# Attention: the four attended tiles of the 13th head's block are split in front of its softmax instead of behind it

## The chip, the cores and the metric

The kernel runs on one core of a Trainium2 chip. The metric is the device time of one execution in microseconds; lower is better. Five engines share the work, and each takes its own instructions strictly in the order in which they were written: PE (TensorE, matrix multiplies, with its weight loads shown as PEld), DVE (VectorE, elementwise), ACT (ScalarE, elementwise with functions), POOL (GpSimd) and SP (SyncE, which here issues DMAs). They wait for each other through semaphores.

## The reference, cut to what matters

Two layers run over a sequence of 1024 positions of width 1024: a gated short convolution with a dense SwiGLU network behind it, then dilated attention with another SwiGLU network. The change touches the attention layer alone.

```
BRANCHES = ((128, 1), (512, 4), (2048, 16))
def dilated_attention_mixer(h, w_qkv, w_out, rel_bias):
    qkv = (h @ w_qkv).reshape(bsz, seq, 3, N_HEADS, HEAD_DIM)
    for window, dilation in BRANCHES:
        o, l = dilated_branch(q, k, v, rel_bias, window, dilation)
    alpha = jax.nn.softmax(jnp.stack(lses, axis=0), axis=0)
    o = jnp.sum(alpha[..., None] * jnp.stack(outs, axis=0), axis=0)
    return o.reshape(bsz, seq, D_MODEL).astype(h.dtype) @ w_out
```

There are 16 heads of 64 columns. The last line, the product of the attended values with `w_out`, is what the four tiles of the change are for.

## The kernel before, in words

Everything is kept transposed: a tile has 128 rows of the model's width and 1024 positions, so eight tiles make the residual stream, and two heads make one tile of attended values. Products are taken to nearly fp32 accuracy from three faster ones: each operand is split into a high part, which ACT rounds off (line 143, `w_hi<-oin` for an attended tile), and a low part, which DVE makes by subtraction (line 144, `w_lo<-oin,w_hi`). PE then multiplies high by high, low by high and high by low (lines 371, 372 and 373).

The attention runs in 17 slots, `slot(n, ...)` for n = 0 to 16. Slot n computes the scores of head n (PE lines 1569 and 1570, with the bias added by DVE in lines 1580 to 1611 and the running maximum `m` in lines 1594 to 1620), hands `m` to POOL, which reduces it over the partitions (line 1623, `mb<-m`), subtracts that maximum from the score tiles on DVE (line 1631) and takes exponentials on ACT (line 1632). The values of head n-1 (PE line 1642, from score tiles `lf`, `lh`, `ld`, `lp` and the value tile `vx`) are computed in the same slot, and ACT evicts their sums (lines 1665 and 1666, `z` and `o`). Between these small products stand dense ones, drawn one by one from a generator by the inner function `other`: first the value projections (`v`, PE lines 1512 to 1514, ACT line 1517), the query and key projections, and at the end `out_product`, the product of `w_out` with the attended tiles 0 to 3.

An attended tile is finished by DVE (line 1707), written to memory by POOL (line 1708, `odram`), and read back by SP into a tile `oin` (line 1793). At the start of slot 12, which is the 13th head's, `load_attended` issues the four loads, and the generator `halves` splits one tile each time that it is advanced; it is given to `slot` as `hook`. The second half of a slot is a loop over eight steps i. In slots up to 13 the softmax (lines 1631 and 1632) is written in step 3, the maximum over the partitions having been asked for at the end of the first half; the copies `kca` of the next head's keys (ACT line 1553) are written in steps 1 and 2.

The value tiles of a group of heads take a detour: ACT evicts `v` (line 1517), POOL writes it to memory (line 1521, `vdram<-v`), and SP reads it back in another layout into the single tile `vx` (lines 1529 and 1531). The last `v` of the last group is evicted in slot 12, and `vx` with its data is first used by the values of head 12 in slot 13. The order of all instructions is written out by hand through these loops; there is no scheduler behind it. Buffers of one page come from a ring of 41.

Of the kernel before, what the change touches and what calls it, by code (L numbers as in the profile page):

```python
# [46 lines left out]
SOFT = 4  # L47
# [52 lines left out]
def trunk(ctx: ExitStack, tc: tile.TileContext, x, gains_in, cwi, ck, cwo, wqkv, wo, relb,  # L100
# [8 lines left out]
    def page(name, dt=F32):  # L109
        return pages.tile([128, 1024], dt, name=name, tag="page", bufs=PAGES)  # L110
# [265 lines left out]
    def run(*gens):  # L376
        for _ in zip(*gens):
            pass
        for g in gens:
            for _ in g:  # L380
                pass
# [1078 lines left out]
    def load_bias(h):  # L1460
        t = scope["pool"].tile([128, L1 + L2], F32, name="bias", tag="bias", bufs=2)
        base = tables.offset + h * G3
        nc.sync.dma_start(t[:, 0:L1], bass.AP(tensor=tables.tensor, offset=base, ap=[[1, 8], [A1, 16], [1, L1]]))
        nc.sync.dma_start(t[:, L1:L1 + L2], bass.AP(tensor=tables.tensor, offset=base + G0,
                                                    ap=[[1, 32], [A2, 4], [1, L2]]))
        return t
# [8 lines left out]
    def attention(norm, qk):  # L1475
# [58 lines left out]
        def load_kq(n):  # L1534

            p, a = divmod(n, 2)
            k, q = qk.kq[p, 1], qk.kq[p, 0]
            rows = lambda t, r: bass.AP(t.tensor, t.offset + r * S, [[S, 64], [1, S]])
            n0, n1 = (slice(64 * i, 64 * i + 64) for i in (a, 1 - a))
            KS[n], QS[n] = page("ka", F32R), page("qa", F32R)  # L1540
            nc.sync.dma_start(KS[n][n0].bitcast(F32), rows(k, 64 * a))
            nc.sync.dma_start(KS[n][n1].bitcast(F32), rows(k, 128 + 64 * a))
            if n <= LAG + 1 and n % 2 == 0 and n:
                load_values(p - 1)
            for m in (n0, n1):
                nc.sync.dma_start(QS[n][m].bitcast(F32), rows(q, 64 * a))
            nc.sync.dma_start(qlo[a][n0].bitcast(F32), rows(q, 128 + 64 * a))

        def classes(n):

            KC[n] = page("kca", F32R)
            for h in range(2):
                nc.scalar.activation(KC[n][:, half(h)], view(KS[n], h * HALF, [[1, 4], [4, 128]]), AF.Copy)
                yield
# [80 lines left out]
        def values(p, a, st):  # L1635
            lf, lh, ld, lp = (st[n] for n in ("lf", "lh", "ld", "lp"))
            acc = [bank(), bank()]
            kd = [[128, 4], [1, 32]]
            b1 = [[32, 16], [1, 8]]

            def mm(ih, off, dims, u, rhs, first=False, last=False):
                nc.tensor.matmul(view(acc[ih], off, dims), vx[:, u, 64 * a:64 * a + 128], rhs,  # L1642
                                 start=first, stop=last)

            for ih in range(2):
                for r4 in range(4):
                    mm(ih, r4 * 32, kd, 8 + r4, view(lf, ih * HALF + r4 * 32, kd), first=r4 == 0)
                    if r4 % 2:
                        yield
            for r4 in range(4):  # L1650
                mm(1, r4 * 32, kd, 12 + r4, view(lh, r4 * 32, kd))
                if r4 % 2:
                    yield
            for j in range(8):
                off = (j % 4) * 8
                mm(j // 4, off, b1, j, view(ld, blk(j), b1), last=False)
                if j:
                    mm(j // 4, off, b1, j - 1, view(lp, blk(j), b1), last=j % 4 == 3)
                yield
            o, z = st["o"], st["z"]  # L1660
            n0 = slice(64 * a, 64 * a + 64)
            z0 = slice(64 - 64 * a, 128 - 64 * a)
            for ih in range(2):
                s = slice(ih * HALF, (ih + 1) * HALF)
                nc.scalar.activation(z[n0, s], acc[ih][z0], AF.Ln)
                nc.scalar.activation(o[n0, s], acc[ih][n0], AF.Copy)
            yield

        def finish(p):

            o, z = OZ.pop(p)
            if p < NPAIR - 1:
                nc.scalar.activation(z, z, AF.Exp, scale=-1.0)
                put_off.append((p, o, z))
                return
                yield

            acts[p] = page("o_hi", F32R), page("o_lo", F32R)

            def scaled(h):  # L1680
                nc.vector.tensor_tensor(out=o[:, half(h)], in0=o[:, half(h)], in1=z[:, half(h)], op=ALU.mult)

            def parts(h):
                split(o[:, half(h)], [t[:, half(h)] for t in acts[p]])

            def rest():
                parts(1)

            nc.scalar.activation(z[:, half(0)], z[:, half(0)], AF.Exp, scale=-1.0)
            scaled(0)  # L1690
            parts(0)
            yield
            nc.scalar.activation(z[:, half(1)], z[:, half(1)], AF.Exp, scale=-1.0)
            scaled(1)
            nc.scalar.activation(scratch, eps, AF.Sqrt)
            yield
            last_part.append(rest)
            yield
            ensure(ahead_ao + KT - AO_WIDE)
            ensure(ahead_ao + KT - AO_WIDE + 4)  # L1700
            yield
# [11 lines left out]
        def slot(n, dense, ndense, late=0, hook=iter(())):  # L1713

            def other(k):
                for _ in range(k):
                    next(dense, None)

            p, a = divmod(n, 2)
            if n < H:  # L1720
                new = dict(bias=bias.pop(n))
                sc = scores(p, a, new)
            else:
                sc = iter(())
            if n + 1 < H:
                load_kq(n + 1)
                bias[n + 1] = load_bias(n + 1)
            if n:
                q, b = divmod(n - 1, 2)
                if b == 0:  # L1730
                    OZ[q] = page("o"), page("z")
                old = live.pop(n - 1)
                old.update(o=OZ[q][0], z=OZ[q][1])
                pv = values(q, b, old)
            else:
                pv = iter(())
            extra = later = iter(())
            lagged = n <= LAG
            if n + 1 < H:
                later = classes(n + 1)  # L1740
            if lagged and a and p:
                ending.append(finish(p - 1))
            used = 0
            if lagged:
                for i in range(8):
                    next(sc, None)
                    if n or i % 2:
                        other(1)
                        used += 1
                    if a and ending and i == 0:  # L1750
                        run(ending.pop())
                run(sc)
            else:
                if a == 0 and not late:
                    other(1)
                    used += 1
                for i in range(8):
                    next(sc, None)
                    next(pv, None)
                    next(pv, None)  # L1760
                    if i >= late and i % 2 == 0:
                        other(1)
                        used += 1
                run(sc)
                run(pv)
                if a == 0:
                    extra = finish(p - 1)
                if a == 0 and n < H:
                    load_values(p)
            left = max(ndense - used, 0)  # L1770
            for i in range(8):
                next(pv, None)
                next(pv, None)
                if i == (2 if n > LAG + 1 else 5):
                    attended()
                if not lagged and (i < FIN0 or i > SOFT):
                    next(extra, None)
                if i in (1, 2):
                    next(later, None)
                if i == (3 if lagged else SOFT):  # L1780
                    if n < H:
                        live[n] = new
                        run(softmax(new))
                if i >= SOFT:
                    next(hook, None)
                other(left * (i + 1) // 8 - left * i // 8)
            run(pv)
            run(extra)
# [45 lines left out]
        def halves():  # L1834
            for q, t in done.items():
                first[q] = split(t)
                yield

        dense = fill()
        for n in range(H):  # L1840
            if n == LAG - 1:
                done.update(load_attended(range(AO)))
            hook = halves() if n == LAG - 1 else iter(())
# [206 lines left out]
```

## Time and profile before

| | us |
|---|---|
| median of 3 runs | 2130.8 (2130.04 to 2131.32) |
| the profiled execution, its own time | 2129.8 |
| its span, from the first to the last instruction | 2128.0 |
| PE busy | 2102.3 (99%) |
| DVE busy | 1739.8 (82%) |
| ACT busy | 1015.7 (48%) |
| POOL busy | 234.4 (11%) |
| mean granted TensorE clock, as a share of full speed | 0.996 |

All views below are of this one execution, and their times are microseconds from its first instruction. A row of the view in order of time gives the start, the duration, the engine, the line, the operation with the tiles it writes and reads, the shapes and how many instructions were merged; in square brackets stands the idle time of the engine ahead of it and what ended that. An engine that is 99% busy can still be slowed: a busy PE may run at half its clock, and the table by stretches shows the clock that was granted.

### The profile page before, as it was taken

The numbers are of one execution on the slowest core, as the hardware profiler recorded it, in microseconds if no ns is written. First come the engines' busy times: TensorE is split into PE (matmuls) and PEld (weight loads), VectorE is DVE, ScalarE is ACT, GpSimd is POOL, SyncE is SP. The second block draws the span as 40 slices with busy tenths as digits, with TensorE's granted clock in tenths as the row PEclk, the third lists the DMA queues.
The fourth block names the chain that finished last, engine by engine and source line by source line (L and its number), as shares of the span: only waits on it lengthen the run. The fifth ranks groups of instructions, "written<-read, shape, count | busy, mean of one in ns | idle before, by whom it ended". The sixth has DMA issues, their size and how long they took to land.

```text
span 2128.0 us, 30922 instructions
## 1 busy us (share of the span) xinstructions
PE 2102.3 (99%) x11082; PEld 1806.5 (85%) x11082; DVE 1739.8 (82%) x3262; ACT 1015.7 (48%) x1861; POOL 234.4 (11%) x335
## 2 busy tenths in 40 slices
PE   9999999999999999999999999999999999999998
PEld 7888888888888888887899999888788888888887
DVE  8898769988888888878967687787998888888876
ACT  7333426443444554445545545554544444456435
POOL 1000000110101000010322322111011101001000
PEclk9999999999999999999999999999999999999999
DMA  7332642323333566351767767745223233358432
GB/s 219 94 94 70 228 134 75 104 100 109 114 101 108 162 208 211 108 168 40 250 208 186 182 182 211 216 164 152 64 85 109 101 108 114 105 195 241 157 95 79
DMA packets 141464, 300.78 MB, mean 141 GB/s; under 512 B 48188, under 2 KB 54414, under 8 KB 141312
## 3 DMA queue, kind: packets, MB, share of 16 engines
q1 hardware_dynamic: 107488, 201.94, 31.5%
q0 software_dynamic: 26192, 82.17, 11.9%
q10 hardware_dynamic: 7632, 14.70, 1.8%
q8 instruction: 88, 1.44, 0.3%
q14 instruction: 64, 0.52, 0.1%
HBM read 208.48 MB, written 82.93 MB: 137 GB/s over the span
## 4 chain that ended last, share of the span: by engine, by line
PE 85%; DVE 7%; ACT 3%; DMA 2%; issue 2%; POOL 1%; SPq 0%; DVEq 0%; ACTq 0%; POOLq 0%
PE bank L574 19%; PE bank L572 19%; PE bank L573 19%; PE bank L373 4%; PE bank L372 4%; PE bank L371 4%; PE bank L664 3%; PE bank L667 3%; PE bank L666 3%; PE bank L1642 2%; POOL mb L1623 1%; PE bank L1512 1%; PE bank L1513 1%; PE bank L1514 1%; DVE w L144 1%
## 5 line engine op out<-in xcount | busy, mean ns | idle before, releaser
L572 PE MATMUL bank<-b,w 128*128 128x512 f32 x1952 | 764.0, 391 | 2.2 <-ACT w L143 1.8
L574 PE MATMUL bank<-b,w 128*128 128x512 f32 x1952 | 762.0, 390 | 3.6 <-DVE w L144 3.5
L573 PE MATMUL bank<-b,w 128*128 128x512 f32 x1952 | 761.4, 390 | 0.4 <-DVE b L883 0.3
L574 PEld LDWEIGHTS bank<-b,w 128*128 128x128 f32 x1952 | 366.9, 188 | 83.9 <-DVE w L144 7.4
L572 PEld LDWEIGHTS bank<-b,w 128*128 128x128 f32 x1952 | 367.2, 188 | 78.9 <-ACT w L143 2.9
L573 PEld LDWEIGHTS bank<-b,w 128*128 128x128 f32 x1952 | 367.1, 188 | 76.3 <-DVE b L883 1.1
L143 ACT ACTIVATE w<-combo 128x512 fp32r<-128x512 f32 (+2 forms) x488 | 249.1, 540 | 230.2 <-DVE combo L191 213.3
L144 DVE TENSOR_TENSOR w<-combo,w 128x512 fp32r<-128x512 f32 (+2 forms) x488 | 277.7, 583 | 37.6 <-ACT w L143 36.9
L578 ACT ACTIVATE part<-bank 128x512 f32<-128x512 f32 x186 | 110.8, 596 | 390.0 <-PE bank L574 386.6
L144 DVE TENSOR_TENSOR w<-raw,w 128x512 fp32r<-128x512 f32 (+2 forms) x342 | 189.5, 576 | 37.5 <-ACT w L143 37.5
L582 DVE TENSOR_TENSOR part<-part,bank 128x256 f32<-128x256 f32 (+1 forms) x366 | 171.5, 500 | 31.1 <-PE bank L574 16.6
L143 ACT ACTIVATE w<-raw 128x512 fp32r<-128x512 f32 (+2 forms) x342 | 166.9, 530 | 44.4 <-PE bank L574 11.5
L371 PE MATMUL bank<-w_hi,w 128*128 128x512 f32 (+1 forms) x400 | 153.4, 384 | 3.8 <-ACT w_hi L143 3.7
L372 PE MATMUL bank<-w_lo,w 128*128 128x512 f32 (+1 forms) x400 | 149.8, 375 | 1.2 <-DVE w_lo L144 1.2
L373 PE MATMUL bank<-w_hi,w 128*128 128x512 f32 (+1 forms) x400 | 149.8, 375 | 0.7 <-DVE w L144 0.7
L493 DVE TENSOR_TENSOR x<-x,bank 128x512 f32<-128x512 f32 (+1 forms) x104 | 66.4, 644 | 62.6 <-PE bank L373 61.4
L802 DVE TENSOR_TENSOR x<-x,bank 128x512 f32<-128x512 f32 x136 | 93.2, 685 | 29.1 <-PE bank L574 29.1
L191 DVE TENSOR_TENSOR combo<-raw 128x512 f32<-128x512 f32 (+1 forms) x172 | 111.7, 649 | 0.0
L371 PEld LDWEIGHTS bank<-w_hi,w 128*128 128x128 f32 x400 | 75.8, 190 | 17.1 <-ACT w_hi L143 3.9
L372 PEld LDWEIGHTS bank<-w_lo,w 128*128 128x128 f32 x400 | 75.9, 190 | 14.9 <-DVE w_lo L144 2.0
L373 PEld LDWEIGHTS bank<-w_hi,w 128*128 128x128 f32 x400 | 75.6, 189 | 14.7 <-DVE w L144 1.6
L565 DVE TENSOR_TENSOR b<-hin,b 128x512 fp32r<-128x512 f32 x126 | 79.7, 689 | 9.3 <-ACT b L564 9.3
(243 smaller groups left out, 3467.1 us busy)
## 6 DMA issues: line engine op xcount, KB each, us to landing
hin<-part SPq DMA_DIRECT2D x126, 256.0 KB
raw<-in_ffn_w_gate SPq DMA_DIRECT2D x44, 512.0 KB
raw<-in_ffn_w_up SPq DMA_DIRECT2D x44, 512.0 KB
part<-sum POOLq DMA_DIRECT2D x72, 256.0 KB, 2.3
raw<-in_ffn_w_down SPq DMA_DIRECT2D x48, 384.0 KB
raw<-in_attn_w_qkv SPq DMA_DIRECT2D x27, 512.0 KB
raw<-in_conv_w_in SPq DMA_DIRECT2D x24, 512.0 KB
part<-part POOLq DMA_DIRECT2D x36, 256.0 KB, 2.4
```

The costliest lines, as they stand in the source:

```text
L143: nc.scalar.activation(hi, src, AF.Copy)
L144: eng.tensor_tensor(out=lo, in0=src, in1=hi, op=ALU.subtract)
L191: eng.tensor_tensor(out=c, in0=a, in1=b, op=op)
L371: nc.tensor.matmul(b, whi[:, a], ahi[:, s], start=first, stop=False)
L372: nc.tensor.matmul(b, whi[:, a], alo[:, s], start=False, stop=False)
L373: nc.tensor.matmul(b, wlo[:, a], ahi[:, s], start=False, stop=last)
L572: nc.tensor.matmul(b, hi[:, a], bhi, start=start and k == 0, stop=False, skip_group_check=True)
L573: nc.tensor.matmul(b, hi[:, a], blo, start=False, stop=False, skip_group_check=True)
L574: nc.tensor.matmul(b, lo[:, a], bhi, start=False, stop=k == n - 1, skip_group_check=True)
L578: nc.scalar.activation(t, b, AF.Copy)
L582: nc.vector.tensor_tensor(out=t, in0=t, in1=b, op=ALU.add)
L802: nc.vector.tensor_tensor(out=X[n][:, half(h)], in0=X[n][:, half(h)], in1=b, op=ALU.add)
```

## The change

In the second half of slot 12 the four splits are no longer written in steps 4 to 7, behind the softmax that is written in step 3, but in steps 0 to 3, and in step 3 ahead of the softmax. `hook` is an empty iterator in all other slots, so nothing else is moved.

```
@@ -1777,12 +1777,12 @@
                     next(extra, None)
                 if i in (1, 2):
                     next(later, None)
+                if i < 4:
+                    next(hook, None)
                 if i == (3 if lagged else SOFT):
                     if n < H:
                         live[n] = new
                         run(softmax(new))
-                if i >= SOFT:
-                    next(hook, None)
                 other(left * (i + 1) // 8 - left * i // 8)
```

PE, POOL and SP execute the same instructions in the same order as before. On ACT, in slot 12, the copies `w_hi<-oin` are the high parts of the four attended tiles, `kca<-ka` the key copies for the next head, line 1632 the exponentials, and `v<-bank,r` the eviction of the last value tile. Before:

```order
L1517 ACTIVATE v<-bank,r 128x256
L1553 ACTIVATE kca<-ka 128x512 x2
L1632 ACTIVATE lf<-lf 128x1024
L1632 ACTIVATE lh<-lh 128x512
L1632 ACTIVATE ld<-ld 128x1024
L1632 ACTIVATE lp<-lp 128x16x24
L1632 ACTIVATE lp<-lp 128x512
L143 ACTIVATE w_hi<-oin 128x1024
L1517 ACTIVATE v<-bank,r 128x256
L143 ACTIVATE w_hi<-oin 128x1024 x2
L1665 ACTIVATE z<-bank 64x512
```

The same place on ACT, now:

```order
L1517 ACTIVATE v<-bank,r 128x256
L143 ACTIVATE w_hi<-oin 128x1024
L1553 ACTIVATE kca<-ka 128x512
L143 ACTIVATE w_hi<-oin 128x1024
L1553 ACTIVATE kca<-ka 128x512
L143 ACTIVATE w_hi<-oin 128x1024 x2
L1632 ACTIVATE lf<-lf 128x1024
L1632 ACTIVATE lh<-lh 128x512
L1632 ACTIVATE ld<-ld 128x1024
L1632 ACTIVATE lp<-lp 128x16x24
L1632 ACTIVATE lp<-lp 128x512
L1517 ACTIVATE v<-bank,r 128x256
```

All four high parts moved ahead of the exponentials, two of them between the key copies; the eviction of `v` now follows the last exponential directly. The fourth high part stood, before, behind the evictions `z` and `o` of head 11's values.

On DVE, at the same place, line 1620 is the last step of the maximum `m` that POOL reduces, line 1631 are the subtractions that need POOL's result `mb`, and line 1580 is the first work on head 13's scores. Before:

```order
L1620 TENSOR_TENSOR m<-m,lp 128x512
L1631 TENSOR_TENSOR lf<-lf,mb 128x1024
L1631 TENSOR_TENSOR lh<-lh,mb 128x512
L1631 TENSOR_TENSOR ld<-ld,mb 128x1024
L1631 TENSOR_TENSOR lp<-lp,mb 128x16x24
L1631 TENSOR_TENSOR lp<-lp,mb 128x512
L144 TENSOR_TENSOR w_lo<-oin,w_hi 128x1024 x4
L1580 TENSOR_TENSOR lf<-bank,bias 128x4x64 x4
```

And now:

```order
L1620 TENSOR_TENSOR m<-m,lp 128x512
L144 TENSOR_TENSOR w_lo<-oin,w_hi 128x1024 x4
L1631 TENSOR_TENSOR lf<-lf,mb 128x1024
L1631 TENSOR_TENSOR lh<-lh,mb 128x512
L1631 TENSOR_TENSOR ld<-ld,mb 128x1024
L1631 TENSOR_TENSOR lp<-lp,mb 128x16x24
L1631 TENSOR_TENSOR lp<-lp,mb 128x512
L1580 TENSOR_TENSOR lf<-bank,bias 128x4x64 x4
```

The four low parts moved from behind the subtractions of the maximum to the place where DVE waits for POOL's reduction.

More of the change, by code (lines that the diff above doesn't have):

```diff
@@ L1779, in slot @@
                     next(later, None)
+                if i < 4:
+                    next(hook, None)
                 if i == (3 if lagged else SOFT):
@@ L1783, in slot @@
                         run(softmax(new))
-                if i >= SOFT:
-                    next(hook, None)
                 other(left * (i + 1) // 8 - left * i // 8)
```

## The prediction

> **What bounds the kernel now.** I read the page's shares first, then who waited for whom on PE, then the rows of PE, ACT, DVE, POOL and SP around the place of the change, and last the granted clock by stretches.
>
> ```profile
> PE 2102.3 (99%) x11082; PEld 1806.5 (85%) x11082; DVE 1739.8 (82%) x3262; ACT 1015.7 (48%) x1861; POOL 234.4 (11%) x335
> ```
>
> PE is the bound of the whole program, so a microsecond counts only if PE idles less or runs at a higher clock. The waits of PE from 1348 us to shortly before the end:
>
> ```profile
> PE bank L371 <- ACT w_hi L143: 3.7, 1, 3.7
> PE bank L574 <- DVE w L144: 1.4, 2, 1.0
> PE bank L372 <- DVE w_lo L144: 1.2, 2, 0.8
> ```
>
> The first and the third are waits for the very splits that the change moves: 4.9 us. Behind them PE hardly waits again for 750 us, so what PE gains or loses here is carried to the end. The rows of PE at this place:
>
> ```profile
> 1348.13 0.39 PE L1642 MATMUL bank<-lp,vx 128*128 128x128 f32 x2
> 1352.24 0.79 PE L371 MATMUL bank<-w_hi,w 128*128 128x512 f32 x1 [3.72 <-ACT w_hi L143]
> ...
> 1358.33 0.28 PE L1569 MATMUL bank<-qa,kca 128*128 128x256 f32 x1
> ...
> 1358.80 0.49 PE L371 MATMUL bank<-w_hi,w 128*128 128x512 f32 x1
> 1360.06 0.50 PE L372 MATMUL bank<-w_lo,w 128*128 128x512 f32 x1 [0.77 <-DVE w_lo L144]
> ```
>
> And the same run of instructions one slot later, where nothing is late (values, one product, eight value matmuls, two products, scores):
>
> ```profile
> 1376.47 0.39 PE L1642 MATMUL bank<-lp,vx 128*128 128x128 f32 x2
> ...
> 1378.98 0.40 PE L371 MATMUL bank<-w_hi,w 128*128 128x512 f32 x1
> 1379.21 0.39 PE L372 MATMUL bank<-w_lo,w 128*128 128x512 f32 x1
> ...
> 1379.67 0.28 PE L1569 MATMUL bank<-qa,kca 128*128 128x256 f32 x1
> ```
>
> The late stretch takes 1358.33 - 1348.13 = 10.20 us, the undisturbed one 1379.67 - 1376.47 = 3.20. That is 7.0 us, more than the waits. The clock explains the rest; in these rows the columns are the stretch, its length, the busy time of PE, PEld, DVE, ACT and POOL, the granted PE clock, and DMA:
>
> ```profile
> 23.20:26.60 3.40, 1.64 (x7) 0.70 (x5) 3.27 (x7) 2.53 (x5) 0.00 (x0) 1.00 0.03 11
> 26.60:30.00 3.40, 3.32 (x8) 2.64 (x9) 3.37 (x7) 3.40 (x5) 0.00 (x0) 0.50 0.01 2
> ...
> 1299.80:1303.20 3.40, 2.52 (x21) 2.53 (x22) 3.37 (x8) 2.50 (x5) 1.08 (x2) 1.00 1.13 277
> 1303.20:1306.60 3.40, 3.40 (x32) 3.40 (x31) 3.37 (x9) 2.54 (x3) 0.54 (x1) 1.00 0.84 292
> 1347.60:1351.00 3.40, 0.92 (x9) 0.72 (x7) 2.69 (x4) 3.24 (x5) 0.00 (x0) 0.99 0.01 1
> 1351.00:1354.40 3.40, 1.69 (x3) 1.10 (x4) 2.10 (x2) 3.40 (x5) 1.56 (x3) 0.50 0.16 36
> 1354.40:1357.80 3.40, 3.40 (x13) 3.02 (x13) 1.49 (x2) 2.51 (x6) 0.61 (x2) 0.50 0.45 125
> ```
>
> The clock is set anew every 3.4 us. After a stretch with 0.92, 1.64 or 1.69 us of PE work it was halved; after one with 2.52 us it was not. So the wait also cost two stretches at half speed.
>
> **The change part by part.** *What PE gets back.* With the splits ready PE would reach the scores 7.0 us earlier. The next wait, for the fourth tile's low part, goes too: from L371 to L372 it is 1360.06 - 1358.80 = 1.26 us against 1379.21 - 1378.98 = 0.23, so 1.0 more. The lead is 8.0 us.
>
> *Are the splits ready?* The rows of ACT, DVE and POOL:
>
> ```profile
> 1340.12 0.47 ACT L1517 ACTIVATE v<-bank,r 128x256 f32<-128x256 f32 x1 [3.13 <-PE bank L1514]
> 1340.49 2.17 ACT L1553 ACTIVATE kca<-ka 128x512 fp32r<-128x512 f32 x2
> 1347.51 1.06 ACT L1632 ACTIVATE lf<-lf 128x1024 f32<-128x1024 f32 x1 [4.86 <-DVE lf L1631]
> ...
> 1351.15 1.04 ACT L143 ACTIVATE w_hi<-oin 128x1024 fp32r<-128x1024 f32 x1
> 1352.09 0.45 ACT L1517 ACTIVATE v<-bank,r 128x256 f32<-128x256 f32 x1
> ```
>
> ```profile
> 1342.12 0.69 DVE L1620 TENSOR_TENSOR m<-m,lp 128x512 f32<-128x512 f32 x1
> 1346.25 1.23 DVE L1631 TENSOR_TENSOR lf<-lf,mb 128x1024 f32<-128x1024 f32 x1 [3.44 <-POOL mb L1623]
> ...
> 1352.22 3.67 DVE L144 TENSOR_TENSOR w_lo<-oin,w_hi 128x1024 fp32r<-128x1024 f32 x3 [1.93 <-ACT w_hi L143]
> ```
>
> ```profile
> 1343.00 3.22 POOL L1623 PARTITION_ALL_REDUCE mb<-m  x1 [9.19 <-DVE m L1620]
> ```
>
> ACT sits idle for 4.86 us and DVE for 3.44 us, both for POOL's reduction. Four high parts at 0.94 (1351.15 to 1352.09) and the key copies of 2.17 end at 1340.49 + 3.8 + 2.2 = 1346.5, ahead of the exponentials: on ACT the move is free, and the key copies end two high parts later, long before PE's scores. On DVE four low parts at 3.67/3 = 1.2 us begin when `m` is done, 1342.8, and end at 1347.7. PE asks for the first at 1348.3 and for one more every microsecond or so, so its wait goes even with some delay. But 4.9 us of work fill a hole of 3.44: the subtraction of the maximum starts at 1347.7 instead of 1346.25, 1.45 late, if the reduction and the low parts do not touch each other.
>
> *They do.* Elsewhere in this trace DVE has run subtractions of the same kind beside that reduction, and these rows price it (duration min/median/max in ns for groups):
>
> ```profile
> 1229.76 3.22 POOL L1623 PARTITION_ALL_REDUCE mb<-m  x1 [6.36 <-DVE m L1620]
> L144 DVE TENSOR_TENSOR w_lo<-raw,w_hi x2: 1214/1774/2334, 1230.4 to 1232.6; 128x1024 fp32r<-128x1024 f32 x2
> ...
> 1291.29 3.21 POOL L1623 PARTITION_ALL_REDUCE mb<-m  x1 [6.39 <-DVE m L1620]
> 1292.39 1.33 DVE L1148 TENSOR_TENSOR kq_lo<-kq,kq_hi 128x512 fp32r<-128x512 f32 x1 [0.70 <-ACT kq_hi L1145]
> L1148 DVE TENSOR_TENSOR kq_lo<-kq,kq_hi x32: 669/685/1331, 1020.2 to 1302.9; 128x512 fp32r<-128x512 f32 x32
> ```
>
> The first low part starts 0.6 us into the reduction and takes 2334 ns instead of 1214: 1.1 lost. The other starts 1.1 us in and takes 1331 instead of 685: 0.65 lost. Both lose what is left of the reduction's first 1.7 us, and the reduction is not longer for it. DVE thus loses between nothing and 1.7 us; I take 1.1, the row with the same shape, because the first low part starts before the reduction does. The subtraction then starts at 1348.8, 2.55 late.
>
> The Trainium skill (SBUF — State Buffer, the section on SBUF's two separate sides) says that a DVE instruction with two SBUF inputs and a GpSimd instruction that reads SBUF take a shared pair of ports as an exclusive lock, and the loser waits for the whole instruction. The rows agree on the conflict, not on its length: the first low part was done at 1232.7, before the reduction's end. What the whole instruction would cost is the first rival.
>
> *What is late next.* Nothing needs head 12's exponentials soon, but the eviction of `v` stands behind them on ACT, and behind it POOL's store, SP's loads of `vx`, and PE's values of head 12 in slot 13:
>
> ```profile
> 1352.84 2.17 POOL L1521 DMA_DIRECT2D vdram<-v  x4 [6.62 <-ACT v L1517]
> 1357.23 0.38 SPq L1529 DMA_DIRECT2D vx<-vdram  x1
> 1357.65 1.68 SPq L1531 DMA_DIRECT2D vx<-vdram  x2
> SPq L1529 <- DMA vdram<-v: 12.1, 1, 12.1
> DMA packets 2284, 0.57 MB, mean 140 GB/s; under 512 B 2284, under 2 KB 2284, under 8 KB 2284
> 1368.79 1.95 PE L1642 MATMUL bank<-lf,vx 128*128 128x128 f32 x16
> ```
>
> SP issues the loads the moment that the stores have landed. PE's first 16 matmuls need the first two loads, 384 KB in rows of 256 bytes, 1536 packets; from 1357.2 to 1361.3 the queue moved 2284, those of the third load and some of the fourth with them. I put the landing at 1361.3, an estimate from that row. Before, that was 7.5 us ahead of PE; it cost nothing. Now `v` is 2.55 later with the softmax and 0.94 earlier, one high part less being ahead of it: 1.6 late, so `vx` lands at 1362.9. PE comes 8.0 earlier, at 1360.8. A new wait of 2.1 us stands there, between 1.0 (if nothing is lost on DVE) and 2.7 (if all 1.7 us are).
>
> *What that wait does to the clock.* It leaves 1.3 us of work in a stretch of 3.4 if it falls into one, and 2.3 or so in the larger part's stretch if it is cut in two. By the rows above the first halves the clock for one stretch, 1.7 us lost, and the second may not. I take 1.7, the likelier.
>
> *The sum.* 8.0 - 2.1 - 1.7 = 4.2 us off the profiled execution's 2129.8: 2125.6. The runs' median lies 1.0 above that execution, so I forecast 2126.6. Behind slot 13, chains move with PE; SP's other loads come 1.6 later, which I cost at nothing because PE's rows show no wait for them and they are used a slot later. Should that cover be gone, PE would wait there instead, up to the whole gain.
>
> **The rivals.** *The reduction blocks the low parts in full.* The first low part delays it to 1344.0, the other three follow at 1347.3 and end at 1350.9; `v` is 4.65 - 0.94 = 3.7 late, `vx` lands at 1365.0, and PE waits 4.2 us, longer than today's 3.72, and loses as much by a halved clock and the start behind it as today: 8.0 - 4.9 (the waits) = 3.1. The gain is 8.0 - 4.2 - 3.1 = 0.7: 2130.1. For it speaks that both subtractions above were held to the same moment of the reduction, as by a lock; against it that the row of 2334 ns ended before the reduction did. Chance 0.12.
>
> *The wait leaves the clock alone.* 8.0 - 2.1 = 5.9: 2124.9. The Trainium skill (TensorE: Matmul & The Clock Gate, its table of goals) asks for no gaps of over about 3 us, and its Part 1 halves the clock after an idle window of about 3.4 us; by that rule a wait of 2.1 us is free. The trace differs: 1.64 us of work in 3.4 were not enough at 23.20. But a wait cut by the border between two stretches escapes. Chance 0.23.
>
> *Nothing is lost on DVE.* Wait 1.0, no clock lost: 7.0 gained, 2123.8. Against it the two rows beside the reduction. Chance 0.12.
>
> *It does not do what it says*: the early splits wait for buffers or for the loads of `oin`, or the lead is used up later; around 2130. Those loads had nearly 20 us, so chance 0.08.
>
> *Slower.* The reduction queues behind all four low parts, in the place where DVE used to idle: it starts at 1347.7 and ends at 1350.9, the softmax is 4.7 late, `vx` lands at 1365.1 as in the first rival, and PE's wait of 4.3 us halves the clock for three stretches instead of two, 5.1 lost: 8.0 - 4.3 - 5.1 = -1.4, 2132.2; two more such stretches, which a second wait close behind would bring, take it past 2135. It decides from the point where `vx` lands later than 1368.8 less what the halved clock costs, some 1364 to 1366. Against it: the reductions above kept 3.2 us beside DVE. The loads behind `vx` on SP could make the second wait. Chance 0.06.
>
> **How the numbers follow.** About 0.2%, 4.3 us, is what a measurement of this kernel can tell from no change: 2126.5 and 2135.1 are the bounds. My forecast, 0.39, lies on the first, so I count 0.17 of it as faster and 0.22 as the same. Faster: 0.17 + 0.23 + 0.12 = 0.52, rounded to 0.5. Slower beyond the bound: 0.05 of the last rival. The rest, 0.45, is the same. The range goes from the case without a loss on DVE, whose wait may also be a little shorter, to the full block: 2123.5 to 2130.3. The forecast's own range, from its bounds of 1.0 and 2.7 for the wait, is 2125.5 to 2127.2.
>
> **What would show it.** Right: PE's 3.72 us and 0.77 us for the splits are gone; the four low parts stand between 1342.8 and about 1348.8 with one or two of them near 2 us; a wait of PE for `vx` at about 1361; one stretch at half clock behind it instead of two before. Wrong: a reduction longer than 3.2 us, a low part that starts only at the reduction's end, no wait for `vx`, or a new wait of PE in slots 14 to 16.

## The result and the profile after

The changed kernel takes 2126.03 us in the median (2123.77 to 2126.98, 11 runs) beside 2130.43 us of the kernel before (2129.76 to 2131.7, 11 runs): a ratio of 0.9975 with a 95% interval of 0.9967 to 0.9983. The time lies 0.6 us under the forecast of 2126.6 us and inside the range; the case "faster" came true, 0.5 us past its bound of 2126.5 us. The profiled execution took 2125.84 us, with a span of 2124.1 us.

The waits of PE in the changed kernel from 1340 us to shortly before the end (line and what was waited for; total us, times, longest):

```profile
PE bank L1642 <- DVE m L1620: 2.1, 1, 2.1
PE bank L574 <- DVE w L144: 1.5, 2, 1.0
```

These are the two longest rows of that view; the others, 1.0, 0.8 and 0.5 us at L1969, L1954 and L664, stand in the kernel before too, the first two of them in the last 11 us of the program. Both waits for the splits, 3.7 us at L371 and 0.8 us at L372, are gone, and one of 2.1 us is new. In the rows of PE it stands here:

```profile
1348.40 0.39 PE L1642 MATMUL bank<-lp,vx 128*128 128x128 f32 x2
1348.55 0.48 PE L371 MATMUL bank<-w_hi,w 128*128 128x512 f32 x1
...
1351.61 0.28 PE L1569 MATMUL bank<-qa,kca 128*128 128x256 f32 x1
...
1363.14 3.31 PE L1642 MATMUL bank<-lf,vx 128*128 128x128 f32 x16 [2.06 <-DVE m L1620]
```

From the last values of slot 12 to the first scores it is 1351.61 - 1348.40 = 3.21 us, as in the undisturbed slot; in the kernel before it was 10.20 here. The new wait stands in front of slot 13's first value products. The row names the running maximum `m` as the releaser, but these products read `lf` and `vx`; what they waited for is tested below.

Now the engines that make the splits and the softmax. DVE first; the second and third row are two narrow looks at the low parts: the first alone, and the first and second merged, which end at 1347.06:

```profile
1342.40 0.69 DVE L1620 TENSOR_TENSOR m<-m,lp 128x512 f32<-128x512 f32 x1
1343.01 1.22 DVE L144 TENSOR_TENSOR w_lo<-oin,w_hi 128x1024 fp32r<-128x1024 f32 x1
1343.01 4.05 DVE L144 TENSOR_TENSOR w_lo<-oin,w_hi 128x1024 fp32r<-128x1024 f32 x2
1349.26 1.21 DVE L1631 TENSOR_TENSOR lf<-lf,mb 128x1024 f32<-128x1024 f32 x1
```

The four as a group, with the least, median and longest duration in ns:

```profile
L144 DVE TENSOR_TENSOR w_lo<-oin,w_hi x4: 1212/1216/2914, 1343.0 to 1348.1; 128x1024 fp32r<-128x1024 f32 x4
```

And POOL, then ACT and SP:

```profile
1343.28 4.04 POOL L1623 PARTITION_ALL_REDUCE mb<-m  x1 [9.21 <-DVE m L1620]
1354.89 2.17 POOL L1521 DMA_DIRECT2D vdram<-v  x4 [7.58 <-ACT v L1517]
```

```profile
1350.50 1.06 ACT L1632 ACTIVATE lf<-lf 128x1024 f32<-128x1024 f32 x1 [3.76 <-DVE lf L1631]
1354.14 0.46 ACT L1517 ACTIVATE v<-bank,r 128x256 f32<-128x256 f32 x1
1359.28 0.38 SPq L1529 DMA_DIRECT2D vx<-vdram  x1
1359.71 1.26 SPq L1531 DMA_DIRECT2D vx<-vdram  x2
```

One low part took 2.91 us instead of 1.21, and the reduction 4.04 us instead of 3.22. The subtraction of the maximum, the exponentials and `v` come late by that, and so do the loads of `vx`.

The granted clock, in stretches of 3.41 us (columns as in the prediction: stretch, length, busy time of PE, PEld, DVE, ACT and POOL, the clock, DMA):

```profile
1356.81:1360.23 3.42, 3.42 (x22) 3.03 (x21) 3.18 (x9) 3.40 (x5) 0.26 (x1) 1.00 0.41 116
1360.23:1363.64 3.41, 1.35 (x8) 0.90 (x7) 2.81 (x6) 0.51 (x1) 0.33 (x1) 1.00 0.92 210
1363.64:1367.05 3.41, 3.41 (x16) 3.27 (x15) 0.00 (x0) 0.00 (x0) 2.90 (x1) 0.50 1.06 263
1367.05:1370.47 3.42, 3.42 (x24) 3.08 (x23) 2.95 (x4) 1.10 (x2) 0.00 (x0) 1.00 0.90 205
```

The wait left 1.35 us of work in its stretch, and the next one ran at half clock: one stretch where before there were two.

**A common measure.** Executions of one kernel differ by some 2 us already in front of the change: the last maximum of slot 12 (the DVE row L1620 above) began at 1342.02 to 1344.20 us in four profiles of the changed kernel. So the table counts each profiled execution from there to its end. "Waits" are PE's at the place of the change; "halved" counts the stretches at half clock directly behind them. The letters are those of the experiments.

| kernel | span | start of that row | from there to the end | PE's waits | halved |
|---|---|---|---|---|---|
| before | 2128.0 | 1342.12 | 785.9 | 3.72 + 0.47 + 0.77 | 2 |
| after | 2124.1 | 1342.40 | 781.7 | 2.06 | 1 |
| after, a2 | 2121.8 | 1342.02 | 779.8 | 1.80 | 0 |
| after, a3 | 2123.9 | 1344.20 | 779.7 | 1.71 | 0 |
| after, a4 | 2122.0 | 1342.41 | 779.6 | 1.68 | 0 |
| a1, `v` first | 2121.6 | 1343.90 | 777.7 | none | 0 |
| a5, `v` first | 2121.0 | 1343.29 | 777.7 | none | 0 |
| b1, older store | 2120.8 | 1343.13 | 777.7 | none | 0 |
| c0, one pass less | 2122.7 | 1343.46 | 779.2 | 1.27 | 0 |
| c1, one pass more | 2124.5 | 1342.38 | 782.1 | 2.49 | 1 |
| c2, two passes more | 2124.9 | 1342.96 | 781.9 | 0.83 + 2.82 | 0 |
| d1, high parts alone | 2126.1 | 1343.83 | 782.3 | 2.71 | 1 |

Take 777.7 us as the time without any wait, add the waits and 1.7 us for each halved stretch: 781.5 for the profile after, 779.5 for a2, 779.0 for c0, 781.9 for c1, 782.1 for d1, 786.1 for the kernel before. All are within 0.3 us of the measured ones; c2, at 781.4, is 0.6 short, of which the experiment below accounts for 0.3.

### The profile page after: what moved, and what is told of

Same layout as the page of the kernel before. It is cut to its first block, busy times and chain, and to the rows that moved or that the text cites. A ratio compares the mean times of both kernels' runs of the same rounds, so it can differ in the third digit from the quotient of the medians.

```text
span 2124.1 us, 30930 instructions
## 1 busy us (share of the span) xinstructions
PE 2099.8 (99%) x11082; PEld 1804.4 (85%) x11082; DVE 1741.0 (82%) x3262; ACT 1017.5 (48%) x1861; POOL 236.0 (11%) x335
## 3 DMA queue, kind: packets, MB, share of 16 engines
q8 instruction: 88, 1.44, 0.3%
## 4 chain that ended last, share of the span: by engine, by line
PE 85%; DVE 7%; ACT 2%; issue 2%; POOL 1%; DMA 1%; SPq 0%; DVEq 0%; ACTq 0%; POOLq 0%
PE bank L574 19%; PE bank L572 19%; PE bank L573 19%; PE bank L371 4%; PE bank L373 4%; PE bank L372 4%; PE bank L1642 3%; PE bank L664 3%; PE bank L667 3%; PE bank L666 3%; PE bank L1512 1%; PE bank L1513 1%; PE bank L1514 1%; DVE w L144 1%; PE bank L1570 1%
## 5 line engine op out<-in xcount | busy, mean ns | idle before, releaser
L371 PE MATMUL bank<-w_hi,w 128*128 128x512 f32 (+1 forms) x400 | 152.8, 382 | 0.1
L372 PE MATMUL bank<-w_lo,w 128*128 128x512 f32 (+1 forms) x400 | 149.2, 373 | 0.0
L371 PEld LDWEIGHTS bank<-w_hi,w 128*128 128x128 f32 x400 | 75.6, 189 | 13.2 <-issue 0.7
L372 PEld LDWEIGHTS bank<-w_lo,w 128*128 128x128 f32 x400 | 75.6, 189 | 12.7 <-issue 0.7
```

The lines of the kernel that those rows point to most:

```text
L371: nc.tensor.matmul(b, whi[:, a], ahi[:, s], start=first, stop=False)
L372: nc.tensor.matmul(b, whi[:, a], alo[:, s], start=False, stop=False)
```

## The experiments

The theory was the prediction's: PE gets the splits in time, the softmax is late because the four low parts overfill the hole on DVE and POOL's reduction holds one of them up, `v` is evicted behind the softmax's exponentials on ACT, and the loads of `vx` are what PE now waits for. Each run below moves one link of that chain. All times are beside the kernel before on the same chip.

**a1: `v` ahead of the exponentials.** The softmax of slot 12 is written in step 5 of the second half instead of step 3. The only effect on the order is that ACT evicts `v` in front of the five exponentials.

```
-                if i == (3 if lagged else SOFT):
+                if i == (5 if n == LAG - 1 else 3 if lagged else SOFT):
```

> The four splits stay ahead of the softmax as in the changed kernel; the eviction of the last v on ScalarE is now ahead of the five exponentials instead of behind them; nothing else is reordered. Theory (PE's 2.06 us wait in slot 13 is for vx, which hangs on that eviction): v is evicted at about 1347 instead of 1354.1, vx lands before 1357, PE does not wait at the first values of head 12 and its clock is not halved: 2.06 + 1.7 us below the changed kernel, 8.0 us below the kernel before, about 2122.3. Rival (the wait is for DVE's maximum m, which the profile names): the wait stays, about 2126. Rival (the lead cannot be carried to the end): the wait goes here and comes back in slots 14 to 16, about 2126.

Measured: 2122.14 us (2121.28 to 2125.02, 5 runs), ratio 0.9963 (0.995 to 0.9975). The rows of ACT, POOL, DVE and PE:

```profile
1348.54 0.47 ACT L1517 ACTIVATE v<-bank,r 128x256 f32<-128x256 f32 x1 [0.30 <-PE bank L1514]
1344.78 4.04 POOL L1623 PARTITION_ALL_REDUCE mb<-m  x1 [9.21 <-DVE m L1620]
1349.31 2.17 POOL L1521 DMA_DIRECT2D vdram<-v  x4 [0.49 <-ACT v L1517]
1344.51 6.32 DVE L144 TENSOR_TENSOR w_lo<-oin,w_hi 128x1024 fp32r<-128x1024 f32 x4
1362.42 1.95 PE L1642 MATMUL bank<-lf,vx 128*128 128x128 f32 x16
```

The reduction is still stretched and the low parts still take 6.3 us, but `v` is evicted 4.6 us behind the maximum's start (1348.54 - 1343.90) instead of 11.7, and PE's row has no wait any more. So the lost time on DVE costs nothing by itself; it costs through `v`. The wait for `vx` was worth what theory said, and this kernel beats both others.

**b1: the loads of `vx` cut loose from `v`.** Everything stays as changed, but the pair's loads read a store of an older pair, so that they need not wait for the late `v`. Heads 12 and 13 are thus computed with another pair's values.

```
-            src = vdram[p // 2]
+            src = vdram[2 if p == 6 else p // 2]
```

> Only the source of one load differs from the changed kernel: the last-but-one pair's vx is read from a store of v that was made long before, so its loads on SP do not stand behind the late eviction of v, while v itself, the exponentials and the low parts stay where they are. The values of heads 12 and 13 are therefore computed with an older pair's v and are not the reference's. Theory (PE's new wait is for vx, and vx is late because of v's store): no wait of PE at slot 13's first value products, POOL's reduction still 4.0 us and the four low parts still 6.3 us together, about 2122.1 us as with v evicted first. Rival (the wait is for the running maximum m on DVE, as the profile's row names it, or for the banks that ACT evicts behind the exponentials): a wait of 1 to 2 us stays and the time is about 2125 to 2126.

Measured: 2122.29 us (2121.58 to 2122.62, 4 runs), ratio 0.996 (0.9945 to 0.9975). SP, POOL and PE:

```profile
1346.71 0.58 SPq L1529 DMA_DIRECT2D vx<-vdram  x1
1344.01 4.04 POOL L1623 PARTITION_ALL_REDUCE mb<-m  x1 [9.17 <-DVE m L1620]
1355.62 2.17 POOL L1521 DMA_DIRECT2D vdram<-v  x4 [7.57 <-ACT v L1517]
1361.66 1.95 PE L1642 MATMUL bank<-lf,vx 128*128 128x128 f32 x16
```

`v` and its store are as late as in the changed kernel (`v` 11.74 us behind the maximum's start, as there), the maximum `m` and the banks are where they were, and PE does not wait. This settles what PE waited for: `vx`. The profile's "DVE m" was an instruction that happened to end last beside it, at 1363.07, 0.07 us ahead of the products. In the profile a2 of the same changed kernel, below, the same wait is put down to the load itself.

**c0, c1, c2: `v` earlier and later by exponential-sized passes.** c0 puts the last two of the softmax's five passes behind `v`; c1 and c2 add one and two idle passes over a 128x1024 tile between the softmax and `v` on ACT.

```
-                if i == (3 if lagged else SOFT):
+                if i == 3 and n == LAG - 1:
+                    live[n], soft = new, softmax(new)
+                    for _ in range(3):
+                        next(soft)
+                elif i == 5 and n == LAG - 1:
+                    run(soft)
+                elif n != LAG - 1 and i == (3 if lagged else SOFT):
```

c1 (c2 has 2 in place of 1):

```
+                        for q in range(1 if n == LAG - 1 else 0):
+                            nc.scalar.activation(done[q], done[q], AF.Copy)
```

> The last two of the five exponentials are moved behind the eviction of v, which is thus about 0.95 us earlier than in the changed kernel. Theory (a stretch of 3.4 us with more than some 2 us of PE work keeps the clock): PE's wait is 1.1 us, the clock is not halved, and the gain over the kernel before is 8.0 - 1.1 = 6.9 us, about 2123.5. Rival (any such wait halves the clock for one stretch): only the 0.95 us are gained over the changed kernel, about 2125.1.

> One more ScalarE pass over 128x1024, which changes no value (a tile is copied onto itself), stands between the exponentials and the eviction of v, which is thus 0.95 us later than in the changed kernel. Theory (vx sets the wait, and the clock is set by stretches of 3.4 us): the wait is 3.0 us, one stretch is halved in every run, and the time is 0.95 to 1.4 us above the changed kernel, 2127.0 to 2127.5. Rival (the wait is not for vx): no change, 2126.0.

> Two such passes, v 1.9 us later than in the changed kernel. Theory: the waits of PE add up to 4.0 us, as long as the wait of the kernel before, and two stretches are halved in most runs: 8.0 - 4.0 - 3.4 = 0.6 us below the kernel before, about 2129.8; with one stretch 2128.1. Rival (the clock is halved once whatever the wait): 1.9 us above the changed kernel, 2127.9. Rival (the wait is not for vx): 2126.0.

Measured: c0 2123.7 us (2122.52 to 2124.47, 5 runs; 0.9967, 0.9955 to 0.998), c1 2126.58 us (2125.78 to 2129.14, 11 runs; 0.9984, 0.9975 to 0.9993), c2 2127.61 us (2125.38 to 2129.48, 11 runs; 0.9988, 0.9979 to 0.9997). The rows of PE with a wait, first c1, then c2:

```profile
1363.80 3.45 PE L1642 MATMUL bank<-lf,vx 128*128 128x128 f32 x16 [2.49 <-DMA vx<-vdram]
```

```profile
1357.10 0.38 PE L1569 MATMUL bank<-qa,ka 128*128 128x256 f32 x1 [0.83 <-ACT v L1517]
1365.63 2.02 PE L1642 MATMUL bank<-lf,vx 128*128 128x128 f32 x16 [2.82 <-DMA vx<-vdram]
```

The wait follows `v`: `v` starts 10.80, 11.74, 12.69 and 13.63 us behind the maximum in c0, the changed kernel, c1 and c2, and slot 13's values start at 19.95, 20.4 to 20.7, 21.42 and 22.67. c0 came out as theory had it; its row puts the wait of 1.27 us down to `m` as well. c1 and c2 are below the times that were expected. The wait I added to, 2.06 us, is the longest of four measured for the changed kernel (1.68, 1.71, 1.80, 2.06), so c1's is 2.49 and not 3.0. In c2 PE already stands for 0.83 us at the scores in front, for a bank that the late `v` still holds. With shorter pauses that the view does not list, PE begins its wait for `vx` 19.85 us behind the maximum in c2 (1362.81 - 1342.96) and 18.93 in c1 (1361.31 - 1342.38), against 18.68 in the changed kernel. So PE lost 1.17 + 2.82 = 4.0 us in c2, as theory had it, and with that sum the table's arithmetic for c2 is within 0.3 us too. What theory had wrong in c2 is the clock: no stretch was halved behind the wait in its profile, although PE stood for 2.82 us, and its median of 2127.61 us lies near the figures for one halved stretch, 2127.9 and 2128.1, and not near that for two, 2129.8.

**a2, a3: the clock behind the same wait.** The changed kernel once more, for two further profiles.

> The changed kernel once more, for the granted clock alone. The transitions of the clock in each profile so far lie a whole number of 3.413 us stretches apart, on a grid whose place differs from execution to execution. Theory (a stretch with less than about 1.4 us of PE's work halves the next one, one with more than about 1.8 us does not, and between the two it goes either way): PE's wait of 2.06 us is the same in this execution, and whether the clock halves behind it follows from where the grid cuts it. If the wait lies whole in one stretch, one halved stretch follows and the time is 2125.5 to 2127; if it is cut so that neither part exceeds 1.6 us, none follows and the time is 2123.7 to 2124.3. Rival (the clock halves behind this wait always, as the prediction had it): a halved stretch there whatever the cut. Rival (differences between executions come from the waits): another length of the wait.

> The same kernel again, for another place of the grid: the same theory and rivals as for the run before it.

Measured: 2123.55 us and 2125.65 us, one run each. PE's wait in a2, then the stretches there, and those of c2 from above:

```profile
1362.51 2.02 PE L1642 MATMUL bank<-lf,vx 128*128 128x128 f32 x16 [1.80 <-DMA vx<-vdram]
```

```profile
1357.98:1361.40 3.42, 2.73 (x15) 1.99 (x13) 3.38 (x9) 2.34 (x3) 0.00 (x0) 1.00 0.45 104
1361.40:1364.81 3.41, 2.30 (x18) 2.27 (x19) 1.26 (x2) 0.00 (x0) 1.87 (x1) 1.00 1.07 243
1364.81:1368.22 3.41, 3.41 (x24) 3.08 (x23) 2.71 (x4) 0.76 (x1) 1.35 (x1) 1.00 1.00 230
```

```profile
1361.31:1364.72 3.41, 1.50 (x7) 0.91 (x6) 3.38 (x8) 1.83 (x2) 0.00 (x0) 1.00 0.52 119
1364.72:1368.14 3.42, 2.51 (x19) 2.46 (x20) 0.05 (x1) 0.00 (x0) 3.12 (x1) 1.00 1.04 246
```

In a2 the border at 1361.40 cuts the wait (1360.71 to 1362.51) in two, neither stretch is short of work, and none is halved: 779.8 us from the maximum to the end against 781.7 in the profile above. The theory had that; its time of 2123.55 us lies just below the 2123.7 that I had named. In c2 a longer wait is cut at 1364.72; 1.50 us of work remained, and the clock stayed. a3 has no halved stretch behind its wait either, but its time is like that of the first profile: it lost the time long before, at 59 us, as PE's row and the stretches there show:

```profile
59.37 0.74 PE L574 MATMUL bank<-b,w 128*128 128x512 f32 x1 [2.04 <-DVE w L144]
```

```profile
56.04:59.45 3.41, 1.36 (x7) 0.83 (x5) 1.98 (x4) 0.63 (x1) 0.00 (x0) 1.00 0.44 153
59.45:62.86 3.41, 3.41 (x8) 2.68 (x9) 3.41 (x7) 1.26 (x2) 0.00 (x0) 0.50 0.48 154
```

So my figure for a3's time, 2123.7 to 2124.3 without a halved stretch at the wait, was wrong as a time of the whole run and right from the maximum on (779.7). With the stretches of 3.41 us laid over all twelve profiles of the table, every stretch at full clock with 0.84 to 1.44 us of PE's work was followed by a halved one (eight of eight, two of them in the last 10 us of the program); those with 1.50 to 2.03 went either way; none above that was. The rival "always" is out; that the wait itself differs between executions holds for up to 0.4 us.

**d1: the high parts alone in front.** ACT's four high parts stay early, the low parts go back behind the subtractions on DVE.

```
+                        if n == LAG - 1:
+                            for q, t in done.items():
+                                nc.vector.tensor_tensor(out=first[q][1], in0=t, in1=first[q][0], op=ALU.subtract)
...
-                first[q] = split(t)
+                first[q] = page("w_hi", F32R), page("w_lo", F32R)
+                nc.scalar.activation(first[q][0], t, AF.Copy)
```

> The high parts stay in front of the softmax on ACT, and the four low parts go back behind it on DVE, right behind the subtractions of the maximum. Theory (the low parts and POOL's reduction stretch each other): the reduction is back at 3.2 us, the subtractions start when it ends, the four low parts take 1.22 us each, 4.9 in all, against 6.3 now. PE then waits about 2.8 us for the first low part, little or nothing for the other three, and not for vx, since v comes some 2.7 us earlier: 8.0 - 2.9 = 5.1 us gained of the time before, less 0 to 1.7 us of halved clock, 2125.0 to 2126.7. Rival (it is ACT's high parts that lengthen the reduction, or the place of the work matters not): the reduction stays at 4.0 us, everything behind is 0.8 us later, and PE's wait is 3.6 us, 2126 to 2127.5.

Measured: 2126.82 us (2124.35 to 2127.85, 10 runs), ratio 0.9979 (0.997 to 0.9989). POOL, DVE and PE:

```profile
1344.71 3.22 POOL L1623 PARTITION_ALL_REDUCE mb<-m  x1 [9.17 <-DVE m L1620]
1347.96 1.23 DVE L1631 TENSOR_TENSOR lf<-lf,mb 128x1024 f32<-128x1024 f32 x1 [3.44 <-POOL mb L1623]
1351.91 4.62 DVE L1788 TENSOR_TENSOR w_lo<-oin,w_hi 128x1024 fp32r<-128x1024 f32 x4
1353.18 0.80 PE L372 MATMUL bank<-w_lo,w 128*128 128x512 f32 x1 [2.71 <-DVE w_lo L1788]
```

With the same high parts on ACT beside it the reduction is back at 3.22 us, and the four low parts take 4.62 us instead of 6.32. So it is the low parts and the reduction that hold each other up, 1.70 us on DVE and 0.82 on POOL, and not ACT. PE now waits 2.7 us for the first low part and not for `vx`: from the maximum on d1 is as long as the changed kernel with its clock halved (782.3 against 781.7), and its median lies 0.1 us above the expected range.

**a4, a5: the changed kernel and `v` first, five rounds side by side.**

> The changed kernel, in five rounds beside the next one, to compare the two on one chip. From the running maximum of slot 12 to the end it should take 781.7 us with a halved stretch behind the wait for vx and 779.7 without; before it was 785.9. Theory (the wait for vx halves the clock in some executions only): runs of both kinds, spread by 2 us and by another 2 us from the first 60 us, which the change does not touch; median 2125 to 2126.

> The kernel that evicts v ahead of the exponentials, again, beside the changed one. Theory (no wait of PE is left between slot 12 and slot 13's values, so the whole lead of 8.0 to 8.2 us is kept): 777.7 us from the running maximum of slot 12 to the end in every execution, median 2122 to 2123, 2 to 4 us below the changed kernel's and 7.5 to 8.5 below the kernel's before. Rival (something later uses up part of the lead): 779 us or more there.

Measured: the changed kernel 2125.51 us (2123.17 to 2126.91, 8 runs), ratio 0.9973 (0.9963 to 0.9983); `v` first 2122.79 us (2121.82 to 2123.51, 5 runs), ratio 0.9961 (0.9947 to 0.9974). From the maximum on a5 took 777.7 us, the same as a1 and b1: nothing later uses up the lead. The two intervals of the ratios overlap, but the profiles differ by 1.9 us or more at the one place where the orders differ, each time.

## Why the prediction was right, point by point

- *The lead of 8.0 us.* Right. Without a wait the program ends 785.9 - 777.7 = 8.2 us earlier from the maximum on (a1, a5, b1). PE reached slot 13's values 1361.08 - 1342.40 = 18.68 us behind the maximum, where the forecast had 1360.8 - 1342.12 = 18.68.
- *The high parts free on ACT, the low parts in DVE's hole.* Right: the first product starts 0.15 us after the last values do (1348.55 and 1348.40). Both waits for the splits are gone.
- *1.1 us lost on DVE, the reduction not longer.* The step was mis-sized in both. DVE lost 1.70 us, the upper bound, and the reduction took 0.82 us more, which stands in the prediction's list as a sign of being wrong. I had taken the row in which a low part starts 0.6 us into a reduction that runs already. Here the first low part was in flight until 1344.23, the reduction stood behind it for 0.82 of its 0.95 us, and the second low part then lost the full 1.7. Even so the subtraction came 2.73 us late by the maximum's start (6.86 - 4.13) instead of 2.55, and `v` 1.77 instead of 1.6. The longer reduction ended at 1347.32, in front of the last low part, so its 0.82 us hid behind DVE. And it was luck that the 4.9 us of the prediction for four low parts were 0.28 too many (4.62 in d1), which hid half of the 0.6 us that were missing.
- *By the Trainium skill* (SBUF — State Buffer, the section on SBUF's two separate sides) the loser of the shared ports waits for the other's whole instruction. These runs agree for the reduction behind a low part, and not for the low part behind the reduction, which was held 1.70 us of 4.04.
- *The new wait of 2.1 us for `vx`.* Right in kind, shown by a1 and b1; the size was 2.06 in the first profile and 1.68 to 1.80 in three others. My landing of `vx` was estimated 0.2 to 0.6 us too late, which in the first profile made up for `v` being 0.17 later than I had it; that the forecast and that profile agree so closely is luck.
- *One stretch at half clock, 1.7 us.* This step failed as a certainty. It is what the first profile shows, one of four, but in a2, a3 and a4 the same wait left the clock alone, which was the rival of 0.23: 781.7 us with it, 779.6 to 779.8 without. Where the 3.41 us stretches lie differs from execution to execution, so the term is a chance and not a sum. The prediction's stretch of 1.69 us was no evidence for it either way, since it ran at half clock itself. The Trainium skill's Part 1 in TensorE: Matmul & The Clock Gate halves the clock after an idle window of about 3.4 us; three of the four profiles agree with that rule, and the first one, c1 and d1 do not, whose waits of 2.06, 2.49 and 2.71 us were shorter than that.
- *Median 1.0 us above the profile.* Not carried over: the first profile of the changed kernel lies 0.2 under its median. It was of the kind with the halved stretch, which may be the reason; the runs without a profile do not show it. That the forecast of 2126.6 is so near to 2126.03 and 2125.51 is partly luck: it rests on two terms, the clock and the offset, that did not hold as they were forecast.
- *The rivals.* "Blocks in full" is out (one low part lost 1.7 us, none waited for the reduction's end), "nothing lost on DVE" is out, and nothing slower came of it.

What stays open: how the clock decides between 1.5 and 2.0 us of work in a stretch, which of the runs without a profile were halved, and why `vx` lands up to 0.4 us later in one execution than in another.

## What to carry to other kernels

When work is moved into the hole in front of a stage, ask what stands behind that stage on the same engine: here the gain of 8.2 us was cut to 4.2 to 6.3 by an eviction queued behind exponentials that nobody needed soon, and writing that eviction first gave it back. A profile's releaser is only the last thing that ended; cutting the suspected dependence (b1) or shifting it in steps (c0 to c2) tells more. Compare executions from a mark just in front of the change: the scatter of the first 60 us, 2.2 us, was as large as what a halved stretch costs.

## What the runs showed of the hardware

- A low part on DVE and POOL's reduction exclude each other only for part of the reduction. The reduction began 0.95 us ahead of the end of a low part and took 4.04 us instead of 3.22; the low part behind that one took 2.91 us instead of 1.21 and was still done 0.26 us ahead of the reduction's end. All ten profiles with the low parts in that place show these durations. What the reduction does in the part that excludes them is not shown.
- A halved stretch does not always cost its 1.7 us. In a2 the clock was halved from 26.78 to 30.19 us, as before the change, and PE then waited only 0.56 us at 58.84; in a3 it was not halved there, PE waited 2.04 us at 59.37 for the same splits, and the stretch behind that was halved. The last maximum of slot 12 came 2.18 us later in a3. What is lost at 26 us is covered by a wait that stands anyway; what is lost at 59 us is not.

The early wait in a2, by PE's row and the halved stretch:

```profile
58.84 0.50 PE L574 MATMUL bank<-b,w 128*128 128x512 f32 x1 [0.56 <-DVE w L144]
```

```profile
26.78:30.19 3.41, 3.41 (x9) 2.63 (x8) 3.38 (x7) 3.41 (x6) 0.00 (x0) 0.50 0.01 2
```
